# First norm's modulation: the last four k-blocks from rows on VectorE, beside the matrix products on TensorE

## The chip, the cores and the metric

The kernel runs on one core of a Trainium2 chip. The metric is device microseconds (us) of one execution, and the kernel before was run three times: 1737.07 us in the median, 1736.29 the lowest and 1737.78 the highest. One further execution was profiled, and all rows of the trace come from that one.

## The reference

One layer of a diffusion backbone: 256 latent tokens `x` and 256 context tokens `ctx`, each of width 2048. What matters here is the very first step. From a conditioning vector `c` (and, for the context stream, `c_ctx`) six modulation vectors of 2048 come out of one large matrix; the first norm is then scaled and shifted by two of them, and everything after reads the result `h` (or `hc`).

```
mod   = silu(c)     @ w_mod + b_mod          # w_mod: 2048 x 12288
mod_c = silu(c_ctx) @ w_mod + b_mod
sh_a, sc_a, ... = split(mod, 6)
h  = rmsnorm(x,   norm_g[0]) * (1 + sc_a)  + sh_a
hc = rmsnorm(ctx, norm_g[0]) * (1 + csc_a) + csh_a
p  = h @ w_in                                 # and so for hc; the mixer's input projection
```

Behind that come attention and a bidirectional recurrence, their merge, an output projection, and a SwiGLU layer, none of which the change touches.

## The kernel before

All values are fp32. Products that need the accuracy are made of three products each: an operand is split into a high part and a low remainder (ScalarE casts the high part, VectorE subtracts it), and high x high, high x low and low x high are summed in PSUM.

Activations lie transposed: 128 channels of the width on the partitions, tokens along the free side. The width of 2048 is thus 16 *k-blocks* of 128 channels. `hx` holds h of both streams for all k-blocks, with high and low part. For k-block k, `make_h` (lines 196 to 203) multiplies x by the scale column `A1[:, k]` and by the norm's factor (line 200, VectorE), adds the shift column `SH1[:, k]` and casts (line 201, ScalarE), and takes the remainder (line 202, VectorE). So h of a k-block can only be made once its two columns of modulation are there.

**The modulation's products.** `w_mod`'s first third (scale and shift of the first norm, 2048 x 4096 words, 33.5 MB) comes as 32 tiles `wm1` of 1 MB, loaded by `load_w` (lines 98 to 101) on SyncE's queue into a pool with three buffers, `raw`. `GROUPS` says how many k-blocks each group makes: four groups of one, then six of two. A group of one has two tiles, a group of two has four. In line 282 TensorE multiplies a tile with the silu of both conditioning vectors as the stationary operand (32 columns of which two are filled), four contraction blocks in four column strips of the array; the result `pm` is a pair of rows. Those rows must become columns: ScalarE copies them out of PSUM (line 297), TensorE turns them with small products (line 300, `pt`), and VectorE adds the bias and makes `A1` and `SH1` (lines 304 to 306).

**The first blocks.** So that TensorE has other work while the modulation weights come in, six output blocks of the next stage's projection are summed along with it, k-block by k-block (`pre`, `pre_mm`, products of line 144): 18 products for a k-block. Their weights `wst` come in pieces, on SyncE's queue for k-blocks 0 to 3 and on GpSimd's from 4 on (line 224), and are split by `start_operands` (lines 244 to 265), which also calls `make_h`. k-blocks whose number leaves a remainder below 3 when divided by 5 have their split weights in the pool `wH`/`wL`, the others in eight buffers `hC`.

The loop over the groups (lines 267 to 310) takes a group's tiles one by one and puts a share of the waiting first-block products behind each; a group's own k-blocks are lined up for later rounds, and two empty rounds at the end take the rest. `norm_x` (lines 184 to 194) makes the norm's factor of a stream: eight squares on ScalarE, summed on VectorE, and a product with ones on TensorE (line 193, `ssx`).

The written order is not the order that runs: each engine takes its instructions strictly in the order of its queue, and this order is drawn up at build time by a planner, which goes by its own idea of costs and lets whatever is ready first go first, the earlier written one before the later one. Buffers are given out in that same plan. Thus the first-block products of a group run in the trace right behind that group's own turn into columns, one round earlier than they are written.

Later in the kernel 64 further tiles of `w_mod` (`wm2`) are worked off on VectorE by `mod_job` (line 346): there the matrix lies with the output channels on partitions, and one instruction multiplies a row of 2048 with the broadcast vector and sums it.

## Time and profile before

| what | before |
|---|---|
| median of three runs | 1737.07 us |
| the profiled execution, its own time | 1737.94 us |
| its span, first to last instruction | 1736.2 us |
| mean granted clock of TensorE | 0.992 |
| TensorE / VectorE / ScalarE busy | 98% / 63% / 44% |
| read from and written to HBM | 376.03 MB / 6.32 MB |
| modulation tiles of 1 MB, first norm | 32, all on TensorE |

How to read it: the span is divided among engines that run at once, each with its own queue. A busy share says how much of the span an engine had an instruction under way, not that it set the time. Names such as `pre<-hx,wH` are what an instruction writes and reads, "L144" is line 144 of the kernel; line 144 is a helper's, so the name tells which products are meant: `pre` is the first blocks in the stage under study, `ps` the projections behind it. In rows of the timeline and of the chain the first number is the start, the second the length; in groups of instructions the number behind the busy time is the mean duration in ns. An fp32 product that isn't split shows as two instructions.

### The profile page before, as it was taken

To read this page: it belongs to the slowest core of one execution; us is meant where nothing else is said; L and a number is where in the kernel's file an instruction comes from. 1 tells how busy PE (TensorE), PEld (TensorE's weight loads), DVE (VectorE), ACT (ScalarE), POOL (GpSimd) and SP (SyncE) were. 2 spreads that over 40 slices of the span, in tenths; PEclk is the share of its full clock that TensorE was granted. 3 is DMA by queue.
4 is the path that set the end of the run, shared out by engine and by line. 5 is a ranking of instruction groups with operands and counts; after the bars stand their busy time and mean duration, and the time that the engine had idled before them with its cause. 6 is when DMAs were issued, how large, how long until landed. Compare 5 with 4: busy or idle time off the path is not lost.

```text
span 1736.2 us, 22132 instructions
## 1 busy us (share of the span) xinstructions
PE 1695.1 (98%) x8715; PEld 1411.1 (81%) x8715; DVE 1087.9 (63%) x1619; ACT 763.8 (44%) x1086; POOL 53.2 (3%) x81
## 2 busy tenths in 40 slices
PE   6899999999999999999999899999999999999997
PEld 4457888888888888889998788888888888888886
DVE  5336877787778776666765765565455655545456
ACT  5225443333334544445544554444444444344443
POOL 0100000000000000001210000000000000000000
PEclk9899999999999999999999999999999999999999
DMA  9983545555556565587766456665566665555553
GB/s 388 357 325 133 198 165 200 213 194 203 186 180 230 186 252 190 194 308 295 266 230 227 158 218 243 242 234 186 194 241 233 236 231 209 193 193 184 213 193 121
DMA packets 60247, 383.78 MB, mean 221 GB/s; under 512 B 7104, under 2 KB 7920, under 8 KB 16880
## 3 DMA queue, kind: packets, MB, share of 16 engines
q1 hardware_dynamic: 55328, 368.15, 57.7%
q0 software_dynamic: 4096, 13.11, 2.0%
q8 instruction: 68, 1.11, 0.2%
q10 hardware_dynamic: 720, 1.12, 0.2%
q14 instruction: 35, 0.29, 0.0%
HBM read 376.03 MB, written 6.32 MB: 220 GB/s over the span
## 4 chain that ended last, share of the span: by engine, by line
PE 96%; DMA 2%; DVE 1%; ACT 1%; issue 0%; SPq 0%; DVEq 0%; ACTq 0%
PE pst L832 45%; PE ps L144 13%; PE ps L148 11%; PE ps L149 6%; PE psb L767 5%; PE pre L144 4%; DMA raw<-in_wm_dram 1%; PE pm L282 1%; PE pst L926 1%; PE psS L705 1%; PE po L729 1%; PE psS L702 1%; PE pv L677 1%; PE pq L661 1%; PE pk L144 1%; PE pgt L968 1%
## 5 line engine op out<-in xcount | busy, mean ns | idle before, releaser
L110 DVE TENSOR_TENSOR wL<-raw,wH 128x1024 fp32r<-128x1024 f32 x480 | 589.1, 1230 | 480.2 <-ACT wH L108 458.9
L108 ACT CAST wH<-raw 128x1024 fp32r<-128x1024 f32 x480 | 502.6, 1048 | 700.0 <-PE pst L832 390.5
L832 PE MATMUL pst<-wH,hx 128*128 128x512 f32 x2272 | 660.6, 390 | 0.0
L832 PEld LDWEIGHTS pst<-wH,hx 128*128 128x128 f32 x2272 | 425.7, 188 | 87.6
L832 PE MATMUL pst<-wL,hx 128*128 128x512 f32 x1136 | 402.2, 389 | 0.0
L148 PE MATMUL ps<-hx,wH 128*128 128x512 f32 x832 | 298.9, 400 | 0.0
L832 PEld LDWEIGHTS pst<-wL,hx 128*128 128x128 f32 x1136 | 213.2, 188 | 44.4
L149 PE MATMUL ps<-hx,wL 128*128 128x256 f32 x832 | 234.9, 283 | 0.0
L144 PE MATMUL ps<-hx,wH 128*128 128x512 f32 x672 | 212.4, 394 | 0.0
L148 PEld LDWEIGHTS ps<-hx,wH 128*128 128x128 f32 x832 | 156.2, 188 | 36.8 <-issue 1.9
L346 DVE CUSTOM_DVE_ANT_0 raw<-raw,cb 128x2048 f32<-128x2048 f32 x64 | 146.1, 2283 | 29.1 <-DMA raw<-in_wm_dram 29.1
L149 PEld LDWEIGHTS ps<-hx,wL 128*128 128x128 f32 x832 | 157.0, 189 | 3.3 <-DVE mx L707 1.1
L144 PEld LDWEIGHTS ps<-hx,wH 128*128 128x128 f32 x672 | 125.2, 188 | 25.5
L144 PE MATMUL ps<-hx,wL 128*128 128x512 f32 x336 | 132.0, 393 | 0.0
L144 PE MATMUL pre<-hx,wH 128*128 128x512 f32 (+1 forms) x204 | 68.7, 420 | 5.5 <-ACT hx L201 5.3
L144 PEld LDWEIGHTS ps<-hx,wL 128*128 128x128 f32 x336 | 63.2, 188 | 12.6
L144 PEld LDWEIGHTS pre<-hx,wH 128*128 128x128 f32 x204 | 40.6, 209 | 26.5 <-ACT hx L201 12.7
L767 PE MATMUL psb<-hx,wH 128*128 128x256 f32 x256 | 46.8, 283 | 0.0
L767 PE MATMUL psb<-hC,wH 128*128 128x256 f32 x256 | 46.8, 283 | 0.0
L767 PEld LDWEIGHTS psb<-hx,wH 128*128 128x128 f32 x256 | 39.9, 192 | 0.0
L767 PEld LDWEIGHTS psb<-hC,wH 128*128 128x128 f32 x256 | 39.9, 192 | 0.0
L144 PE MATMUL pre<-hx,wL 128*128 128x512 f32 (+1 forms) x102 | 39.5, 390 | 0.0
(258 smaller groups left out, 1416.6 us busy)
## 6 DMA issues: line engine op xcount, KB each, us to landing
raw<-in_wm_dram SPq DMA_DIRECT2D x96, 1024.0 KB, 4.8
raw<-in_wfi_dram SPq DMA_DIRECT2D x88, 1024.0 KB, 4.8
raw<-in_win_dram SPq DMA_DIRECT2D x73, 1024.0 KB, 4.8
raw<-in_wfo_dram SPq DMA_DIRECT2D x44, 1024.0 KB, 4.8
raw<-in_wbr_dram SPq DMA_DIRECT2D x16, 1024.0 KB, 5.5
raw<-in_wout_dram SPq DMA_DIRECT2D x16, 1024.0 KB, 4.8
raw<-in_wqk_dram SPq DMA_DIRECT2D x4, 1024.0 KB, 5.5
sgd<-sgx POOLq DMA_DIRECT2D x16, 256.0 KB, 5.2
```

What stands on the lines that cost most here:

```text
L108: nc.scalar.copy(H, raw[:, o:o + n])
L110: nc.vector.tensor_tensor(L, raw[:, o:o + n], H.bitcast(F32), op=ALU.subtract)
L144: nc.tensor.matmul(o, l, r, start=(first and i == 0), stop=(last and i == len(seq) - 1))
L148: nc.tensor.matmul(ps, w[0], act.rearrange("p e t -> p (e t)"), start=first, stop=False)
L149: nc.tensor.matmul(ps[:, 0:T], w[1], act[:, 0, :], start=False, stop=last)
L282: nc.tensor.matmul(pm[32 * (k % 4):32 * (k % 4) + 32, 0:n], cst[:, k], raw[:, kk * n:(kk + 1) * n], start=(k < 4), stop=(k >= KD - 4))
L346: nc.vector.tensor_tensor_reduce(out=raw, in0=raw, in1=cbt[0], scale=1.0, scalar=0.0, op0=ALU.mult, op1=ALU.add, accum_out=mod2[:, i // KD ...
L661: nc.tensor.matmul(pq[:, i * T:(i + 1) * T], l, r, start=(k == 0 and i == 0 and z == 0), stop=(k == 3 and i == 1 and z == 2))
L677: nc.tensor.matmul(pv[:, i, :], ckvs[:, k, l, ts_], r, start=(i == 0 and k == 0 and z == 0), stop=(i == 1 and k == 1 and z == 2))
L702: nc.tensor.matmul(psS, qn[a][:, i * T + qb * P:i * T + (qb + 1) * P], kn[b], start=(n == 0), stop=False)
L767: nc.tensor.matmul(ps[:, br * T:(br + 1) * T], l, r, start=(br == 0 and k == 0 and z == 0), stop=(br == 1 and k == NH - 1 and z == 2))
L832: mm = nc.tensor.matmul(ps[hf], l, r, start=(k == 0 and n == 0), stop=(k == nk - 1 and n == 2))
```

## The change

The last four k-blocks (12 to 15) of the first norm's modulation leave TensorE. `GROUPS` ends after eight groups, and `KV = 12` is the first k-block done the other way. Their eight tiles (scale and shift, four k-blocks each) are laid out with the output channels on the partitions, so that VectorE can multiply each row with the broadcast vector and sum it, for both streams, in four pieces of 512 columns.

For that the two conditioning vectors must lie on all partitions. `make_creps` makes these copies at the beginning: 32 products with the identity, whose stationary operand is a column of the vector broadcast over 128 columns, and eight copies out of PSUM, by turns on ScalarE and VectorE. The copies take all eight `hC` buffers until the last tile is reduced. So the split weights of k-blocks 3, 4, 8 and 9 go to the space in `hx` that belongs to the k-blocks 13 to 15, which are made last, and the squares of the second norm go to three slices of another tile instead of `hC` buffers.

A tile is loaded and reduced by `vector_mod` behind the last two tiles of each of the groups 3 to 6, and after group 6 `vector_mod_end` sums the four pieces and writes the columns of `A1` and `SH1`. k-blocks 12 and 13, then 14 and 15, are started in two more empty rounds behind group 7. The number and size of the loads stay as they were.

```
-GROUPS = [1, 1, 1, 1, 2, 2, 2, 2, 2, 2]
+GROUPS = [1, 1, 1, 1, 2, 2, 2, 2]
+KV = 12
...
     def norm_x(s):
...
-            sq = acc if q == 0 else ap.tile([P, 512], F32, tag="hC", name="sqx", bufs=8)
+            if q == 0:
+                sq = acc
+            elif s == 0:
+                sq = ap.tile([P, 512], F32, tag="hC", name="sqx", bufs=8)
+            else:
+                o = 512 + (q - 1) % 3 * 512
+                sq = cst_t[:, o:o + 512]
...
+    creps = []
+
+    def make_creps():
+
+        for s in range(2):
+            for q in range(4):
+                ps = pj.tile([P, 512], F32, tag="pj", name="pcr")
+                for i in range(4):
+                    nc.tensor.matmul(ps[:, i * P:(i + 1) * P], cv[:, 4 * q + i, s:s + 1].broadcast_to([P, P]), ident,
+                                     start=(i == 0), stop=(i == 3))
+                t_ = ap.tile([P, 512], F32, tag="hC", name="crep", bufs=8)
+                if q % 2:
+                    nc.vector.tensor_copy(t_, ps)
+                else:
+                    nc.scalar.copy(t_, ps)
+                creps.append(t_)
+
+    vparts = wk.tile([P, 64], F32, name="vparts").rearrange("p (j s q) -> p j s q", j=8, s=2)
+
+    def vector_mod(j):
+
+        raw = load_w(wm1[2 * KV + j])
+        junk = wk.tile([P, 512], F32, tag="f", name="vjunk")
+        for s in range(2):
+            for q in range(4):
+                r = raw[:, q * 512:(q + 1) * 512]
+                nc.vector.tensor_tensor_reduce(
+                    out=r if s else junk, in0=r, in1=creps[4 * s + q], scale=1.0, scalar=0.0, op0=ALU.mult,
+                    op1=ALU.add, accum_out=vparts[:, j, s, q:q + 1])
+
+    def vector_mod_end():
+        m = wk.tile([P, 16], F32, name="vmod")
+        nc.vector.tensor_reduce(m, vparts.rearrange("p j s q -> p (j s) q"), axis=mybir.AxisListType.X, op=ALU.add)
+        m = m.rearrange("p (k a s) -> p k a s", k=4, a=2)
+        nc.vector.tensor_tensor(A1[:, KV:KD, :], m[:, :, 0], bc(bm[:, KD + KV:2 * KD], 2), op=ALU.add)
+        nc.vector.tensor_tensor(SH1[:, KV:KD, :], m[:, :, 1], bc(bm[:, KV:KD], 2), op=ALU.add)
+        nc.vector.scalar_tensor_tensor(A1[:, KV:KD, :], A1[:, KV:KD, :], 1.0, bc(gsm[:, 0, KV:KD], 2),
+                                       op0=ALU.add, op1=ALU.mult)
...
     norm_x(0)
+    make_creps()
+    pre += [pj.tile([P, 512], F32, tag="pj", name=f"pre{i}") for i in range(4)]
+    pre += [px.tile([P, 512], F32, tag="px", name=f"pre{i}") for i in range(4, NPRE)]
...
+        elif k < KV:
+
+            u = [hx[:, k % 5 - 3, 13 + i] for i in range(3)]
+            pr_ = [(wide(u[0]), wide(u[1])), (u[2][:, 0], u[2][:, 1])]
+            for rw, (H_, L_) in zip(parts, pr_):
+                nc.scalar.copy(H_, rw)
+                nc.vector.tensor_tensor(L_, rw, H_.bitcast(F32), op=ALU.subtract)
...
-    for g, nk in enumerate(GROUPS + [0, 0]):
+    for g, nk in enumerate(GROUPS + [0, 0, 0, 0]):
...
             for _ in range(min(share, len(todo))):
                 pre_mm(*todo.pop(0))
+            if 3 <= g < 7 and kt >= nt - 2:
+                vector_mod(2 * (g - 3) + kt - nt + 2)
         todo, held = held, []
         if not nk:
+            k = KV + 2 * (g - len(GROUPS))
+            for kk in range(k, min(k + 2, KD)):
+                held.extend(start_operands(kk))
             continue
...
             (todo if g < 2 else held).extend(start_operands(k))
+        if g == 6:
+            vector_mod_end()
```

The host lays the eight tiles out behind the others, scale before shift for each k-block.

More of the change, by code (lines that the diff above doesn't have):

```diff
@@ L203, in make_h @@
                                            op0=ALU.add, op1=ALU.subtract)
+    creps = []
[30 more added lines that the diff above has]
+                                       op0=ALU.add, op1=ALU.mult)
     NPRE = 6
-    pre = [pj.tile([P, 512], F32, tag="pj", name=f"pre{i}") for i in range(4)]
-    pre += [px.tile([P, 512], F32, tag="px", name=f"pre{i}") for i in range(4, NPRE)]
+    pre = []
     def pre_mm(ws, k, b, s=None):
@@ L1064, in _layout @@
         k0 += nk
+    for k in range(k0, KD):
+        for base in (D, 0):
+            grp.append(wm[:, base + P * k:base + P * (k + 1)].T[None])
     o["wm1"] = np.concatenate(grp)
```

2 lines of the change are left out of this document (added).

## The prediction

> **What bounds the kernel now.** I read the page first, then the busy time of each engine in stretches of 20 us (every column is a busy time with a count, and at the end stand the granted clock, the share of the DMA engines and their rate), then the chain of waits in order of time.
>
> ```profile
> PE 1695.1 (98%) x8715; PEld 1411.1 (81%) x8715; DVE 1087.9 (63%) x1619; ACT 763.8 (44%) x1086; POOL 53.2 (3%) x81
> ```
>
> ```profile
> 20.00:40.00 20.00, 18.30 (x158) 13.60 (x162) 12.81 (x27) 8.51 (x18) 2.28 (x4) 0.91 1.02 416
> 40.00:60.00 20.00, 15.78 (x96) 8.99 (x92) 11.60 (x30) 9.28 (x22) 6.37 (x12) 0.95 1.01 411
> 60.00:80.00 20.00, 18.33 (x88) 10.67 (x81) 6.57 (x18) 4.31 (x10) 2.13 (x4) 0.84 0.85 320
> 80.00:100.00 20.00, 19.18 (x101) 11.47 (x100) 6.33 (x17) 4.89 (x11) 2.13 (x4) 0.95 0.84 321
> 100.00:120.00 20.00, 19.94 (x111) 11.51 (x110) 6.51 (x17) 5.12 (x11) 0.00 (x0) 1.00 0.81 315
> 120.00:140.00 20.00, 17.51 (x93) 11.85 (x92) 9.59 (x24) 6.00 (x11) 1.19 (x2) 0.92 0.84 331
> 140.00:160.00 20.00, 20.00 (x100) 16.31 (x100) 8.71 (x9) 8.21 (x12) 0.71 (x1) 1.00 0.23 86
> ```
>
> TensorE carries the kernel, and from 140 us on it has no hole at all, so whatever the first stage ends earlier the whole kernel ends earlier. The stage that the change touches ends where the first product of the next one (line 148) starts:
>
> ```profile
> 146.52 0.39 PE L144 MATMUL pre<-hx,wL 128*128 128x512 f32 x1
> 146.74 0.39 PE L148 MATMUL ps<-hx,wH 128*128 128x512 f32 x1
> ```
>
> Until 60 us this stage goes at the pace of the transfers (share 1.0, 411 to 416 GB/s); from 60 to 140 TensorE is nearly full and the transfers run at some 320 GB/s. They have room left there because their three buffers are held by waiting products: the queue's own waits are on the modulation products of line 282.
>
> ```profile
> SPq L100 <- PE pm L282: 82.9, 32, 6.6
> ```
>
> So before the change two resources take turns: the transfers first, TensorE after them. The change takes from the second.
>
> **The change part by part.** The chain in order of time (start, length, what) prices TensorE's side:
>
> ```profile
> 112.08 5.48 PE pre L144 x23
> 118.61 4.93 DMA raw<-in_wm_dram
> 123.59 1.06 PE pm L282 x8
> 124.66 6.80 PE pre L144 x29
> 131.46 1.00 PE pm L282 x8
> ...
> 134.28 0.80 PE pt L300 x8
> 135.49 0.50 DVE xt L200
> 136.01 0.92 ACT hx L201 x2
> 136.98 9.93 PE pre L144 x36
> ```
>
> *Removed.* Eight weight tiles lose their products: 1.0 us each (131.46), 8 us. Two groups lose their turn of the rows (line 300): 0.8 us each (134.28), 1.6 us. Together 9.6 us of TensorE. The row copies on ScalarE go too, worth nothing alone, for ScalarE is at a quarter of its time here.
>
> *What stays.* 29 products took 6.80 us, 0.2345 us each. A k-block is 6 blocks times 3 products, so 18 x 0.2345 = 4.2 us.
>
> *Added at the beginning.* 32 small fp32 products, each shown by the trace as two instructions (the ssx products, two in the code, are four in the row). The nearest rows, with start, length and count:
>
> ```profile
> 12.89 2.07 PE L193 MATMUL ssx<-acc,cn 128*128 128x256 f32 x4 [12.89 <-DVE acc L190]
> ...
> 38.16 0.50 PE L300 MATMUL pt<-c,row 128*128 128x2 f32 x4
> ```
>
> Half an ssx instruction, 0.26 us at that place, is the upper bound for 128 columns, a pt instruction, 0.125 us, the lower one: 64 instructions are 8 to 16.6 us. I take 14, for the ssx row has the full width and the same cold start. The vector they read is copied for TensorE at 4.55 us in the rows of VectorE:
>
> ```profile
> 4.55 0.19 DVE L164 COPY cst<-sm 128x32 f32<-128x32 f32 x1
> ```
>
> From 4.6 us TensorE idles until 12.89: 8.3 us are free, and the norm's product comes up to some 6 us late (0 to 8.3; 0 if it goes ahead of the small ones). Does that cost? The chain says what lay behind it:
>
> ```profile
> 14.96 3.04 PE pm L282 x32
> 18.02 11.15 DMA raw<-in_wm_dram
> ```
>
> The load issued at 18.02 when the first products gave their buffer back took 11.15 us to land, while the page's median for these loads is 4.8:
>
> ```profile
> raw<-in_wm_dram SPq DMA_DIRECT2D x96, 1024.0 KB, 4.8
> ```
>
> 6.3 us of queue stood before it. A delay of 6 us is thus covered by transfers that are due anyway; one of 8.3 costs 2. I put it at 0, with 2 as the upper bound. The eight copies out of PSUM (four on ScalarE, four on VectorE) wait beside the squares and sums of the first norm:
>
> ```profile
> L190 DVE TENSOR_TENSOR acc<-acc,sqx 128x512 f32<-128x512 f32 x14 | 9.7, 692 | 1.9 <-ACT sqx L188 0.7
> L462 ACT COPY vn<-pv 128x512 f32<-128x512 f32 x8 | 4.7, 594 | 1.5 <-PE pv L459 1.5
> ```
>
> At 0.69 and 0.59 us they add at most 2.8 and 2.4 us in front of that norm, under the same cover. The second norm's squares go through three buffers where there were eight: ScalarE then follows VectorE's sums, nothing late. The weights of k-blocks 3, 4, 8 and 9 go to other space of the same number of slots: nothing.
>
> *Added on VectorE.* Each of eight tiles is read twice, in four pieces of 512 columns: 64 passes. The same operation at full width:
>
> ```profile
> L346 DVE CUSTOM_DVE_ANT_0 raw<-raw,cb 128x2048 f32<-128x2048 f32 x64 | 146.1, 2283 | 29.1 <-DMA raw<-in_wm_dram 29.1
> L346 DVE DVE_READ_ACCUMULATOR2_ANT mod<- 128x1 f32 x64 | 5.3, 83 | 0.0
> ```
>
> A quarter of 2283 ns is the lower bound, 0.57 us; L190's 0.692 with the 0.083 of the sum's read is the upper one, 0.775. I take 0.65, near L190, the row of the same width: 5.2 us a tile, 41.6 in all (36.5 to 49.6). In 40 to 120 us VectorE was busy 11.60 + 6.57 + 6.33 + 6.51 = 31.0 us. With 41.6 it is 72.6 of 80. It fits, with little left: a tile's passes can stand in front of a group's scale vectors and h on VectorE's queue, TensorE waits for these h with the next modulation products queued behind, and SyncE's loads wait for the buffers of both. GpSimd's loads of first-block weights wait for VectorE's splits and slip with them; they run several k-blocks ahead.
>
> *Moved.* The transfers are as many bytes, but the eight tiles now go between the others, so the last tile for TensorE is still the 32nd of 32, and behind it stand six k-blocks (10 to 15) where two stood. That is the price: six are 6 x 4.2 = 25.3 us. With the last turn and restart I count 27 us from the end of the last modulation product X to the stage's end, where before it was 146.74 - 132.46 = 14.3.
>
> *When is X?* The thirteenth tile came at about 59.1 us before, waited for by TensorE:
>
> ```profile
> 59.20 1.93 PE L282 MATMUL pm<-raw,cst 128*32 128x512 f32 x8 [2.14 <-DMA raw<-in_wm_dram]
> ```
>
> The transfers were full until then, so it comes no earlier after. GpSimd had four pairs of first-block weights still to issue, the first and the last of them:
>
> ```profile
> 67.86 1.06 POOL L224 DMA_DIRECT2D rw<-in_wst_dram  x2 [9.30 <-DVE wL L110]
> ...
> 92.44 1.06 POOL L224 DMA_DIRECT2D rw<-in_wst_dram  x2 [4.28 <-DVE wL L249]
> ```
>
> From there, 19 tiles of 1.049 MB and four k-blocks of first weights of 0.39 MB (128 x 768 words) are 21.5 MB: at 411 GB/s 52 us. TensorE has 14 tiles, three turns and six k-blocks (4 to 9): 14 + 2.4 + 25.3 = 42 us. Three buffers: thirteen tiles for TensorE hold one for 4.8 + 1.0 us, six for VectorE for 4.8 + 5.2, in sum 135 us, 45 for each buffer before any waiting. So transfers bound it, VectorE and the buffers close by. Before, the slowest resource in this stretch was TensorE: 20 tiles, four turns and 173 products (ten k-blocks less seven) are 20 + 3.2 + 40.6 = 63.8 us, and it took 132.46 - 59.2 = 73.3, 15% more. With the same 15%, 52 become 59.8 and X = 119.
>
> TensorE's work in this stretch leaves it some 17 us idle, and the vector k-blocks are ready once the 28th tile is reduced, four loads before X. I let 3 us of their products slip in ahead of X (0 to 6). End: 119 + 27 - 3 = 143, against 146.74: **3.7 us less**. The rest of the kernel is unchanged and follows TensorE.
>
> The profiled execution took 1737.94 us with a span of 1736.2, 0.87 above the median of 1737.07. 1737.07 - 3.7 = **1733.4 us**. A difference under 0.2%, 3.5 us, counts as none.
>
> **The rivals.**
>
> *The transfers stay full (20%).* For it: 411 to 416 GB/s for 40 us when nothing held them. Then X = 59.2 + 52 + 1 = 112.2, 1 us slips in ahead, the end is 138.2: 8.5 us less, 1728.6. Against it: six tiles now hold a buffer for twice as long.
>
> *VectorE's passes become the wait (18%), slower.* The place is a group's turn in groups 4, 5 and 6: h waits for a tile's whole 5.2 us ahead of it on VectorE, TensorE waits for h, both kinds of buffer stay held, and the transfers stand. Three times 5.2 on the 52 are 67.6 us, X = 127, the end 127 + 27 - 3 = 151: 4.3 us more, 1741.4. It decides once X passes 146.7 - 24 = 122.7, a hold of 3.8 us a group. For it: 72.6 of 80 us busy on an engine that takes its work in order. Against it: a group's own VectorE work is short, and a tile's eight passes needn't stand together.
>
> *The beginning gives it back (15%), no difference.* The small products go first at 0.26 us each: the norm's product 8.3 us late, 2 us of it uncovered, and nothing slips in ahead of X: -3.7 + 2 + 3 = 1.3 us more, 1738.4.
>
> *The transfers' 315 to 321 GB/s after 60 us are their own limit (5%), slower.* 21.5 MB at 320 are 67 us, X = 127, the end 151, 4 us more. Against it: the 411 of the stretch before, and the queue's waits on line 282.
>
> The Trainium skill, DMA: Bandwidth & Descriptors, Specifications, puts the HBM limit of one core at about 358 GB/s; by it 21.5 MB would take an estimated 60 us, with the 15% 69, X = 128, and the change would lose some 5 us; the trace disagrees, with 416 and 411 GB/s in 20 to 60 us, and so this rival has no more than its 5%.
>
> **A cold clock** is a cost inside all of them. After the wait of 2.14 us at 59.20 and after 1.91 at 136.98 the next products ran at half pace:
>
> ```profile
> 61.06 3.36 PE L144 MATMUL pre<-hx,wH 128*128 128x512 f32 x7
> ```
>
> 36 products from 136.98 took 9.93 us instead of 8.4, 1.5 lost. TensorE will idle more in the new stretch; four such losses are 6 us on its 42, still under the 52, so I add nothing.
>
> **How the numbers follow.** The forecast has 42%, with its own range from 1730.4 to 1736.4 by the 0 to 6 us that slip in ahead; what lies beyond 3.5 us in it, rather more than half, is 23%, the other 19% count as no difference. The full transfers add 20% to faster, the late beginning 15% to no difference; of VectorE's rival 15% are slower and 3% no difference, and the transfers' own limit is slower. Faster 43%, no difference 37%, slower 20%. The range of 1727.5 to 1741 leaves out the far ends of the full transfers and half of the two slower rivals.
>
> **What would show it.** The first line 148 product near 143 us; DMA share above 0.9 and TensorE clearly under 18 of 20 us in 60 to 110; 25 us of unbroken line 144 products before the end; passes of 0.6 to 0.7 us; the first ssx product at 13 to 21 us with the transfers still full behind it. I am wrong if TensorE waits for h behind VectorE's passes in groups 4 to 6 (then the second rival), if the transfers are still at 320 GB/s while TensorE idles, or if the last modulation product comes after 122.7 us.

## The result: 1.4% slower

| | before | after |
|---|---|---|
| median, runs | 1737.42 us, 4 | 1761.96 us, 4 |
| lowest to highest | 1736.29 to 1737.99 | 1761.3 to 1763.9 |
| the profiled execution, its span | 1736.2 us | 1759.1 us |
| last modulation product ends | 132.46 us | 139.46 us |
| first projection product (`ps`) | 146.74 us | 169.40 us |

The ratio is 1.0144, its 95% interval 1.0126 to 1.0161: 24.5 us lost where 3.7 were to be won, and outside the range. In the profile the first `ps` product comes 22.7 us later and the span is 22.9 us longer, so the whole loss arises in the stage that the change touches.

The page of the changed kernel gives no hint of it: TensorE's share is a point lower.

```profile
PE 1703.9 (97%) x8699; PEld 1422.8 (81%) x8699; DVE 1128.2 (64%) x1749; ACT 764.2 (43%) x1088; POOL 54.9 (3%) x81
```

The stretches of 20 us do; their columns are as before, the last three being the granted clock, the DMA engines' share and GB/s:

```profile
20.00:40.00 20.00, 16.94 (x122) 12.45 (x126) 12.69 (x25) 8.07 (x17) 3.33 (x6) 0.83 0.95 366
40.00:60.00 20.00, 15.57 (x96) 10.62 (x92) 16.95 (x53) 5.84 (x14) 2.21 (x5) 0.83 0.84 311
60.00:80.00 20.00, 8.42 (x42) 4.09 (x35) 11.11 (x34) 3.44 (x8) 3.12 (x6) 0.62 0.97 388
80.00:100.00 20.00, 14.38 (x69) 7.72 (x67) 11.79 (x35) 2.54 (x5) 2.13 (x4) 0.84 0.68 256
100.00:120.00 20.00, 16.35 (x74) 8.98 (x74) 14.76 (x47) 4.14 (x9) 1.06 (x2) 0.77 0.86 322
120.00:140.00 20.00, 16.71 (x76) 9.16 (x76) 17.57 (x52) 7.65 (x17) 1.06 (x2) 0.83 0.82 299
```

TensorE is busy 8.42 of 20 us in 60 to 80 and never over 17. That would be as forecast if the transfers were full beside it. In 60 to 80 they nearly are, with 388 GB/s; after that they are not: 256 GB/s in 80 to 100, less than before the change. And in 20 to 60, where they ran at 416 and 411 GB/s before, they now run at 366 and 311. VectorE isn't full either, with 11 to 18 of 20 us. No engine bounds this stretch; something that all of them wait for does.

The same view over one stretch, from 20 us to the first `ps` product, for the kernel before and then for the changed one:

```profile
20.00:146.74 126.74, 115.77 (x658) 73.57 (x659) 53.41 (x130) 40.21 (x85) 14.80 (x26) 0.93 0.86 339
```
```profile
20.00:169.40 149.40, 115.64 (x578) 75.58 (x579) 91.96 (x257) 38.81 (x82) 14.82 (x26) 0.82 0.75 287
```

This is the balance of the change. 80 products went (8 tiles of 8 and 2 turns of 8), the forecast's 9.6 us. Yet TensorE is busy just as long, 115.64 against 115.77 us: the clock fell from 0.93 to 0.82, and the products that stayed took 9.5 us longer. Idle time rose from 10.97 to 33.76 us, by 22.8. So -9.6 of work, +9.5 of cold clock, +22.8 of idleness make +22.7.

Two places of idleness. The chain of waits of the changed kernel, start, length and what:

```profile
59.39 1.90 PE pm L340 x16
...
61.31 9.93 DMA raw<-in_wm_dram
...
71.28 1.98 PE pm L340 x8
...
77.69 7.62 PE pre L145 x24
...
90.48 1.04 PE pm L340 x8
91.52 0.02 issue
91.54 8.06 DMA raw<-in_wm_dram
...
99.62 0.69 DVE vjunk L238
...
105.72 2.93 PE pre L145 x6
...
115.08 1.04 PE pm L340 x8
116.12 0.02 issue
116.14 5.31 DMA raw<-in_wm_dram
...
121.47 0.69 DVE vjunk L238
```

The three loads were issued late, behind a modulation product that gave its buffer back, and are waited for to their landing. The first is the fourth tile of group 4 and is TensorE's. The other two are VectorE's tiles, and the chain goes on through their first passes, which stand on VectorE's queue in front of that group's scale vectors or h. The end of the stage, in the rows of TensorE:

```profile
138.40 1.06 PE L340 MATMUL pm<-raw,cst 128*32 128x512 f32 x8
140.23 1.05 PE L363 MATMUL pt<-c,row 128*128 128x2 f32 x8 [0.76 <-ACT row L360]
143.19 3.35 PE L145 MATMUL pre<-hx,wH 128*128 128x512 f32 x7 [1.91 <-ACT hx L208]
...
169.40 0.39 PE L149 MATMUL ps<-hx,wH 128*128 128x512 f32 x1
```

29.9 us from the end of the last modulation product to the next stage, with all 108 first-block products of six k-blocks in it.

Why are the loads late? The SyncE queue's own waits up to 145 us (in total, times, longest), and the rows of the tile `raw` between 59.2 and 139.5 us:

```profile
SPq L101 <- PE pm L340: 53.3, 22, 5.8
SPq L101 <- DMA raw<-in_wm_dram: 26.8, 9, 6.3
SPq L101 <- DVE vparts L238: 24.6, 5, 10.2
SPq L101 <- DVE A L367: 6.2, 1, 6.2
```
```profile
L101 SPq DMA_DIRECT2D raw<-in_wm_dram x19: 327/328/350, 60.5 to 130.6; - x19
...
DMA to landing us min/median/max: 4.7/6.9/10.3
```

19 loads in 70.1 us, 3.9 us apart: with three buffers, one turn of a buffer from a load to the next is 11.7 us. The same rows of the kernel before:

```profile
L100 SPq DMA_DIRECT2D raw<-in_wm_dram x17: 327/328/328, 61.2 to 122.2; - x17
...
DMA to landing us min/median/max: 4.6/5.7/8.7
```

17 loads, 3.8 us apart. The pace of the loads, which the change was to speed up, stayed the same, while two more of them fell into the stretch.

### The profile page after: what moved, and what is told of

The parts are those of the page before. It is cut to its first block, busy times and chain, and to the rows that moved or that the text cites. A ratio compares the mean times of both kernels' runs of the same rounds, so it can differ in the third digit from the quotient of the medians.

```text
span 1759.1 us, 22238 instructions
## 1 busy us (share of the span) xinstructions
PE 1703.9 (97%) x8699; PEld 1422.8 (81%) x8699; DVE 1128.2 (64%) x1749; ACT 764.2 (43%) x1088; POOL 54.9 (3%) x81
## 4 chain that ended last, share of the span: by engine, by line
PE 95%; DMA 2%; DVE 1%; ACT 1%; issue 0%; SPq 0%; DVEq 0%; ACTq 0%
PE pst L897 45%; PE ps L145 13%; PE ps L149 11%; PE ps L150 6%; PE psb L832 5%; PE pre L145 4%; DMA raw<-in_wm_dram 1%; PE pm L340 1%; PE pst L991 1%; PE psS L770 1%; PE po L794 1%; PE psS L767 1%; PE pv L742 1%; PE pq L726 1%; PE pk L145 1%; PE pgt L1033 1%
## 5 line engine op out<-in xcount | busy, mean ns | idle before, releaser
L411 DVE CUSTOM_DVE_ANT_0 raw<-raw,cb 128x2048 f32<-128x2048 f32 x64 | 146.1, 2282 | 29.7 <-DMA raw<-in_wm_dram 29.5
L145 PE MATMUL pre<-hx,wH 128*128 128x512 f32 (+1 forms) x156 | 51.1, 411 | 6.9 <-ACT hx L208 6.9
L145 PEld LDWEIGHTS pre<-hx,wH 128*128 128x128 f32 x156 | 31.4, 211 | 18.7 <-ACT hx L208 9.4
L340 PE MATMUL pm<-raw,cst 128*32 128x256 f32 (+1 forms) x256 | 29.7, 570 | 16.1 <-DMA raw<-in_wm_dram 16.1
```

The costliest lines, as they stand in the source:

```text
L145: nc.tensor.matmul(o, l, r, start=(first and i == 0), stop=(last and i == len(seq) - 1))
L340: nc.tensor.matmul(pm[32 * (k % 4):32 * (k % 4) + 32, 0:n], cst[:, k], raw[:, kk * n:(kk + 1) * n], start=(k < 4), stop=(k >= KD - 4))
L411: nc.vector.tensor_tensor_reduce(out=raw, in0=raw, in1=cbt[0], scale=1.0, scalar=0.0, op0=ALU.mult, op1=ALU.add, accum_out=mod2[:, i // KD ...
```

## Theories and experiments

*Theory*: the three buffers bound the stretch (landing, waiting in an engine's queue, use), and TensorE, in its fixed order, idles, and its clock falls; the end and the beginning add their own loss. *Rivals*: VectorE's passes alone; TensorE's order drawn up by the planner; the small products at the beginning.

All runs, with the profiled execution's end of the last modulation product, first `ps` product, and TensorE's busy and idle time from 20 us to it (busy from the row of the stretches, idle the rest). The ratio is to the kernel before, run again beside each batch of kernels. Its medians there lie between 1737.42 and 1738.88 us, so two rows of different batches can differ by up to 1.5 us for that alone. The last columns come from one execution each: that of e11 took 3.9 us more than its median, that of e19 2.5 more, that of e15 1.5 less.

| kernel | median us | ratio to before, 95% | last `pm` | first `ps` | busy, idle |
|---|---|---|---|---|---|
| after | 1761.96 | 1.0126 to 1.0161 | 139.5 | 169.40 | 115.6, 33.8 |
| e1_own_buffers | 1752.54 | 1.0063 to 1.0096 | 130.1 | 160.31 | 113.1, 27.2 |
| e2_two_passes | 1758.42 | 1.0096 to 1.0126 | 134.9 | 164.88 | 113.9, 31.0 |
| e6_short_hold | 1759.34 | 1.0105 to 1.0135 | 136.2 | 167.37 | 115.8, 31.6 |
| e7_own_two_passes | 1745.84 | 1.0034 to 1.0064 | 124.2 | 154.12 | 111.6, 22.6 |
| e3_copies_alone | 1743.45 | 1.0017 to 1.0041 | 137.8 | 152.18 | 117.9, 14.3 |
| e11_moved_alone | 1739.70 | 1.0007 to 1.0024 | 135.6 | 151.50 | 116.7, 14.8 |
| e4_interleaved | 1747.36 | 1.0035 to 1.0065 | 138.2 | 155.52 | 112.7, 22.9 |
| e9_interleaved_three | 1758.59 | 1.0106 to 1.0132 | 149.2 | 166.27 | 118.2, 28.1 |
| e8_interleaved_own | 1743.45 | 1.0020 to 1.0044 | 133.6 | 150.41 | 107.8, 22.6 |
| e13_own_two_interleaved | 1745.30 | 1.0028 to 1.0052 | 134.9 | 153.86 | 113.8, 20.1 |
| e12_late_copies | 1742.74 | 1.0016 to 1.0039 | 135.9 | 149.96 | 113.9, 16.1 |
| e10_two_blocks | 1757.88 | 1.0098 to 1.0132 | 143.0 | 166.82 | 118.3, 28.5 |
| e14_even_order | 1760.22 | 1.0113 to 1.0147 | 140.5 | 170.10 | 113.9, 36.2 |
| e18_inter_even | 1746.21 | 1.0027 to 1.0061 | 137.5 | 154.78 | 108.8, 25.9 |
| e19_own_even | 1748.69 | 1.0048 to 1.0078 | 128.2 | 159.26 | 116.9, 22.3 |
| e15_own_inter_even | 1736.11 | 0.9981 to 1.0003 | 125.7 | 142.99 | 106.8, 16.2 |
| e16_own_inter_even_late | 1741.83 | 1.0010 to 1.0028 | 132.1 | 149.16 | 113.4, 15.7 |
| e17_before_even | 1736.96 | 0.9988 to 1.0007 | 129.3 | 144.28 | 114.8, 9.5 |

### Buffers or passes

**Own buffers.** Seven of the eight VectorE tiles go to space that is free by then (slices of `cst_t` and `kr`, and the first quarter of both `xs`), each in two loads; the second stays in `raw`.

```
-        raw = load_w(wm1[2 * KV + j])
+        raw = load_own(j)
```

> The changed kernel, but seven of the eight vector tiles are loaded into two buffers of their own (a free slice with the space of kr, and the first k-blocks of x once their h is made), so that the three raw buffers serve TensorE's tiles; VectorE's passes are the same. Theory 'buffers' (a vector tile keeps one of three buffers for 5 to 10 us after landing, and the transfers stand): the last modulation product comes at 115 to 122 us instead of 139.4, DMA share above 0.9 from 60 to 110 us, 1735 to 1745 us in all against 1762. Rival 'VectorE's queue' (its passes stand in front of the groups' h, whoever owns the buffers): within 5 us of the changed kernel, 1757 to 1762.

**Fewer passes**: one piece of the four is multiplied and summed. **Short hold**: all eight passes run, but only the first of each tile reads it.

```
-            for q in range(4):
+            for q in range(1):
```

> The changed kernel with two of the eight passes on each vector tile; the other six are left out, and their part of the modulation with them. Loads and products stay. 'Buffers' and 'VectorE's queue' both expect most of the loss back: 1735 to 1742 us. Rival 'order' (eight tiles loaded between the others and six k-blocks left for the end cost it, whatever VectorE does): 1752 to 1762.

```
-                    out=r if s else junk, in0=r, in1=creps[4 * s + q], scale=1.0, ...
+                    out=junk, in0=creps[7 - 4 * s - q] if s + q else r, in1=creps[4 * s + q], scale=0.0 if s + q else 1.0, ...
```

> The changed kernel, but only the first of the eight passes reads the vector tile; the other seven are made on the resident copies of the vectors and scaled by zero, so that the tile's buffer is free after one pass while VectorE is as busy as before. It leaves out seven eighths of the vector k-blocks' modulation. 'Buffers': 1735 to 1745 us, the queue's waits on the passes nearly gone. 'VectorE's queue': 1755 to 1762 us, since 4.9 us of passes a tile still stand on it.

Own buffers give 9.4 us back, a quarter of the passes 3.5, the short hold 2.6 (10.9, 5.0 and 4.1 against the kernel before of their own batch). None met the theory of the buffers as it was expected: e1 lies between the theory's range and the rival's, e2 in the range of "order", e6 in that of VectorE's queue. So VectorE's passes alone are not the cause, neither by the time that they hold a buffer nor by their work; sharing the buffers is the larger part, and one remedy alone doesn't bring the loss back.

The edits of e1 and e2 in one kernel:

> Buffers of their own for the vector tiles and only two of the eight passes (the other six and their part of the modulation are left out). Theory 'loads held in two ways' (three buffers too few, then VectorE too full): both are lifted, the last modulation product comes at 113 to 120 us, the transfers stay above 390 GB/s to 110 us, and with six k-blocks behind it the total is 1737 to 1743. Rival 'TensorE's order' (its own tiles wait behind a k-block's products whatever VectorE does): the last product at 126 us or later, 1748 to 1753.

Both together: 16.1 us, more than 9.4 and 3.5, and the last modulation product ends at 124.2 us, 5 us from the forecast's 119 and behind the 113 to 120 expected; the time lies between the two ranges. With buffers and passes lifted the stretch up to that product runs nearly as forecast; still this kernel is 8 us slower than before, for the end behind that product stays 30 us.

### The beginning

The small products, copies and moved buffers with all 32 tiles on TensorE, as before the change:

```
-GROUPS = [1, 1, 1, 1, 2, 2, 2, 2]
+GROUPS = [1, 1, 1, 1, 2, 2, 2, 2, 2, 2]
...
-            if 3 <= g < 7 and kt >= nt - 2:
-                vector_mod(2 * (g - 3) + kt - nt + 2)
```

> All sixteen k-blocks on TensorE as before, plus the small products, the eight copies and the moved buffers of the change; no vector tile. Theory 'the beginning is free' (the transfers cover the small products): within 3 us of the kernel before. Rival 'the beginning costs': the transfers fall from 416 to about 366 GB/s in 20 to 40 us as in the changed kernel, and the stage ends 5 us later or more.

The same without the small products and copies (left out of e3):

```
-    make_creps()
```

> This kernel is e3_copies_alone without the small products and their eight copies: all 32 modulation tiles are on TensorE as before the change, only the moved buffers of the change remain (the second norm's squares in three slices, the split weights of k-blocks 3, 4, 8 and 9 in the space of h). Theory that the 5 us at the beginning come from the small products and copies, which change the order that the planner draws up for the groups behind them: 1736.5 to 1738.5 us, as before the change, first projection product (ps) at 146 to 148 us and the fifth modulation tile used at about 29 us. Rival, that the moved buffers cost it (fewer slices for the squares, so the second norm is late): 1741 to 1744 us, as e3_copies_alone, with the fifth tile at 33 to 34 us.

The beginning costs 5.5 us with the small products and 1.7 without (ratios 1.0029 and 1.0016, whose intervals overlap a little), so neither theory was right alone: the moved buffers have a small part, the products and copies probably the larger one. How they cost it shows in the fifth modulation tile. The first row is of `e11_moved_alone`, where it stands behind the second turn as before the change; the second of `e3_copies_alone`, where it stands behind 18 first-block products:

```profile
28.94 1.07 PE L339 MATMUL pm<-raw,cst 128*32 128x256 f32 x16 [0.35 <-DMA raw<-in_wm_dram]
```
```profile
33.49 1.07 PE L340 MATMUL pm<-raw,cst 128*32 128x256 f32 x16
```

Its buffer comes free 4.5 us later, and the transfers, at 416 and 411 GB/s before the change, run at 360 and 365:

```profile
20.00:40.00 20.00, 16.57 (x126) 11.72 (x126) 12.66 (x25) 8.10 (x18) 3.33 (x6) 0.91 0.96 360
40.00:60.00 20.00, 17.71 (x108) 9.78 (x108) 9.47 (x24) 7.10 (x16) 5.15 (x10) 0.91 0.97 365
```

### The end

k-blocks 12 to 15 are started one by one, each behind the group in which its two tiles are reduced.

```
-        if g == 6:
-            vector_mod_end()
+        if 3 <= g < 7:
+            vector_mod_end(g - 3)
+            held.extend(start_operands(KV + g - 3))
```

> The changed kernel with the vector k-blocks finished one at a time, k-block 12 behind group 3 and so on, so that their products stand between the groups and two k-blocks instead of six are left for the end; three raw buffers as in the changed kernel. 'Buffers': the last modulation product stays near 139 us, but only some 14 us follow it instead of 30, so 1744 to 1750. 'VectorE's queue': four h's more between the passes, the last modulation product moves to 145 us or later, 1750 to 1760. If neither holds and the end alone costs ('order'): 1738 to 1744.

In this kernel h of the k-blocks from 13 on overwrites split weights of k-blocks 3 and 4, in part before their products; the amount and kind of the work are the same. The next one puts these weights elsewhere. In both, and in all kernels below that start VectorE's k-blocks one by one, the split weights from k-block 5 on are all in `wH`/`wL`.

> This kernel is the changed kernel with k-blocks 12 to 15 started one by one behind groups 3 to 6, as soon as their two tiles are reduced, instead of all behind the last group; the three buffers stay shared. It differs from e4_interleaved only in the place of the split weights of k-blocks 3 and 4. Theory that the end alone is worth 14 us: 1746 to 1749 us, first ps at 154 to 157, some 17 us from the last modulation product to it. Rival, that what is put ahead at the end only fills TensorE where the loads wait and X moves later by as much: 1755 us or more.

14.6 us back in the one, 3.4 in the other, which differs from it in the place of two weights. For the second the theory failed and its rival held: the last modulation product moves to 149.2 us. Its queue waits for the small closing sums (29.6 us in total, 12.2 in e4) in place of the passes:

```profile
SPq L101 <- PE pm L343: 54.3, 21, 6.1
SPq L101 <- DVE vmod L247: 29.6, 4, 10.2
SPq L101 <- DMA raw<-in_wm_dram: 25.6, 11, 6.7
```

The place also decides which products must wait for which h. With it the planner draws up another order, on VectorE and on TensorE alike, and a tile's buffer then comes free later. These two kernels don't show the order apart from the place; the even order below does, on the second of them.

Interleaving (starting the k-blocks one by one) with the own buffers of e1, and that with the one piece of e2 besides:

> Vector k-blocks finished one at a time behind groups 3 to 6, and seven of the eight vector tiles in buffers of their own; the whole computation. If the two remedies add up (9 us from the buffers, 15 from the end): 1735 to 1740. If VectorE, busy 18.5 of 20 us with the own buffers, then sets the pace: 1742 to 1750.

> This kernel is e8_interleaved_own with two passes per VectorE tile instead of eight (a quarter of each row is multiplied and summed, the other three quarters are left out). It lifts both holds and the end. Theory of three separate losses (beginning 5 us, holds, end): only the beginning is left, the last modulation product ends at 124 to 128, first ps at 142 to 147, 1734 to 1738 us. Rival, that with the end interleaved TensorE's own work and its order set the time, so that the passes no longer matter: as e8_interleaved_own, 1742 to 1745 us.

Interleaved with own buffers: 1743.5 us. With a quarter of the passes besides: no better, against the theory of three separate losses. It seems that without the even order below what is saved in one place is given back in another. e8's time lies where it was expected if VectorE set the pace, but e15 below is faster with VectorE just as busy (18.23 of 20 us in 60 to 80 in both), so VectorE didn't set it.

```
-    make_creps()
...
+            if g == 3 and kt == 0:
+                make_creps()
             if 3 <= g < 7 and kt >= nt - 2:
```

The results of the small products also move to another pool of PSUM (`px` for `pj`).

> This kernel is e8_interleaved_own with the small products and copies written in the middle of the group loop, just ahead of the first VectorE tile, instead of the beginning; they run between first-block products. Theory that their place at the beginning cost 5 us: the fifth modulation tile comes at about 30 to 31 us, the first ps product 4 to 5 us earlier than in e8_interleaved_own, at 145 to 147, 1736 to 1739 us in all, no different from before the change. Rival, that it is their work on TensorE, some 10 us wherever it stands, once TensorE is the slower side: no earlier than e8_interleaved_own, 1743 to 1746 us.

The small products written in the middle of the loop bring nothing that can be measured (1742.7 against 1743.5): the fifth tile is at 31.29 us, near the 30 to 31 expected, but the 32 products, TensorE's and the copies' work, now stand among the first-block products.

```
-GROUPS = [1, 1, 1, 1, 2, 2, 2, 2]
-KV = 12
+GROUPS = [1, 1, 1, 1, 2, 2, 2, 2, 2]
+KV = 14
```

> Only k-blocks 14 and 15 by VectorE: four vector tiles, one in each of the groups 3 to 6, nine groups on TensorE, four k-blocks behind the last modulation product. 'The end' (what stands behind the last product costs 4.2 us a k-block, half as many more as in the change) and a loss in proportion: 1748 to 1752. 'Buffers': one vector tile a group leaves two for TensorE all the time, and most of the loss goes: 1739 to 1744.

Two k-blocks on VectorE instead of four lose 20 us, nearly as much as four, and more than either theory expected. The loss isn't proportional to the moved work.

### The order on TensorE

What was left was the order. In the queue of the changed kernel up to 24 first-block products stand in front of a modulation tile (in others up to 38). One rule keeps the first-block products behind the tile that they are written behind, and a group's own are written one round earlier:

```
+                with tc.issue_after(mm.ins):
                     pre_mm(*todo.pop(0))
...
-            (todo if g < 2 else held).extend(start_operands(k))
+            todo.extend(start_operands(k))
```

> This kernel is the changed kernel with one more rule for the order of TensorE's queue: the first-block products that are written behind a modulation tile aren't put in front of it, and a group's own first-block products are written one round earlier. So 6 to 9 of them, 18 at most, stand between two modulation tiles of a group instead of up to 32. From 20 us to the first ps product the changed kernel takes 149.4 us, of which TensorE is busy 115.6 and idle 33.8. Theory that long runs of first-block products in front of a modulation tile hold its buffer, so that loads start late and TensorE idles later: idle falls by 8 us or more, first ps at 156 to 162 us, 1749 to 1755 us in all. Rival, that the three buffers are held by landing and VectorE's passes whatever TensorE's order: idle within 4 us of 33.8, first ps at 165 to 172, 1758 to 1764 us.

> This kernel is e8_interleaved_own (own buffers for VectorE's tiles, its k-blocks started one by one) with the even order of e14_even_order: first-block products aren't put in front of the modulation tile ahead of which they weren't written. Theory that the planner's uneven order is what is left there: TensorE's idle time from 20 us to the first ps product falls from 22.6 to 14 to 18 us, first ps at 143 to 147, 1735 to 1739 us. Rival, that the order only moves the idle time about: 148 to 152 us, 1741 to 1746 us.

> This kernel is e15_own_inter_even with the small products and copies written in the middle of the group loop, as in e12_late_copies, so that the first groups run as before the change. Theory that order and beginning add up: first ps at 141 to 145 us, 1732 to 1737 us in all, at least as fast as before the change. Rival, that the small products between first-block products put back what their absence at the beginning gives: 145 to 150 us, 1738 to 1743 us.

> This kernel is the kernel before the change with the even order alone; all 32 modulation tiles stay on TensorE. It is the control for the even order: what order alone does without the change. Before, TensorE idles 11.0 us from 20 us to the first ps product, at 146.74. Theory that an uneven order costs where buffers are the narrow place, and less where TensorE is nearly full: first ps at 143 to 148 us, 1734 to 1739 us. Rival, that an even order is a gain or a loss of its own of the same size as in the changed kernel: under 1732 or over 1742 us.

> This kernel is e15_own_inter_even with the three buffers shared again: VectorE's k-blocks started one by one, even order on TensorE, no own buffers. Theory that with three shared buffers neither order nor an interleaved end can help much, since landing and passes hold the buffers (e14_even_order: nothing from the order alone): first ps at 155 to 167 us, between e4 and e9, 1747 to 1759 us. Rival, that order and interleaved end are enough and own buffers are not needed: 143 to 149 us, 1736 to 1741 us.

> This kernel is e15_own_inter_even with VectorE's four k-blocks all behind the last group again, as in the change: own buffers and even order, no interleaving. Theory that the end is then the narrow place: the last modulation product comes at 118 to 124 us, about where the forecast put it, the first ps product some 30 us later, at 147 to 153, 1740 to 1746 us. Rival, that the order brings as little as in e14_even_order: last modulation product at 129 to 131 and first ps at 158 to 161 us, as in e1_own_buffers, 1750 to 1753 us.

By itself the even order brings next to nothing (e14, 1760.2), as its rival said, and nothing to the kernel before either (e17). It helps most where VectorE's k-blocks are started one by one: 12.4 us with three buffers (e9, 1758.6, to e18, 1746.2) and 7.3 us with own buffers (e8, 1743.5, to e15, 1736.1); with own buffers and the k-blocks at the end it is 3.9 us (e1 to e19). So with three buffers, too, the order is part of the loss. The traces of the kernels with three buffers show where (worked out as in the table of the next section): from landing to use TensorE's tiles waited 4.3 us in the mean in e9 and 1.8 in e18, but in the changed kernel 2.5 and in e14 1.5, where landing took 0.5 us longer. The eight kernels with each of the three remedies or without it:

| median us | VectorE's k-blocks at the end | one by one |
|---|---|---|
| planner's order, three buffers | 1762.0 | 1758.6 |
| planner's order, own buffers | 1752.5 | 1743.5 |
| even order, three buffers | 1760.2 | 1746.2 |
| even order, own buffers | 1748.7 | 1736.1 |

In the planner's order both other remedies together give 18.5 us, and starting one by one alone only 3.4. With the even order they add up: own buffers are worth 11.5 and 10.1 us, starting the k-blocks one by one 14.0 and 12.6, both 24.1. Each does it at its own place: own buffers bring the last modulation product from 140.5 to 128.2 and from 137.5 to 125.7; starting one by one brings the `ps` product from 29.7 to 17.3 and from 31.0 to 17.3 us behind it. e18 came just under the theory's range of 1747 to 1759. For e19 it named the right place, the end, but the last modulation product came at 128.2, behind the 118 to 124 expected, and the kernel 3 us over its range.

In `e15_own_inter_even` the forecast's picture stands, from 20 us to the first `ps` product and in 60 to 100 us:

```profile
20.00:142.99 122.99, 106.75 (x578) 68.87 (x579) 93.35 (x269) 37.66 (x82) 14.83 (x26) 0.92 0.86 342
...
60.00:80.00 20.00, 14.79 (x66) 7.59 (x65) 18.23 (x61) 3.20 (x7) 1.46 (x3) 0.74 1.02 418
80.00:100.00 20.00, 20.00 (x104) 13.19 (x103) 18.64 (x59) 6.00 (x13) 2.13 (x4) 1.00 1.02 420
```
```profile
124.62 1.07 PE L356 MATMUL pm<-raw,cst 128*32 128x512 f32 x8
...
142.99 0.39 PE L149 MATMUL ps<-hx,wH 128*128 128x512 f32 x1
```

Transfers full at 418 and 420 GB/s, VectorE at 18 of 20 us beside them, the same 578 products of TensorE in 106.75 us where the changed kernel took 115.64, and the first `ps` product at 143. It is the fastest form of the change, 25.9 us better than the change as made, and not measurably better than the kernel before (0.9992, 0.9981 to 1.0003), nor than the kernel before with the even order alone (e17, 1736.96 in the same batch). The late copies, on top of it, lose 5.7 us: e16's theory fell.

## Why the prediction was wrong, point by point

**The bound of the kernel** was read rightly in effect. "No hole at all" is too strong (TensorE idles 5.5 us between 146.74 and 1720 us before the change), but what the stage lost the kernel lost, 22.7 of 22.9 us.

**Removed, 9.6 us**: right. 80 products fewer, and at nearly the clock of before (e15, 0.92 against 0.93) TensorE needs 106.75 us where it needed 115.77.

**Beginning, cost 0 (0 to 2)**: the size of the work was overrated, its cost missed. The products took 10.3 us, not 14, and the first `ssx` product came at 15.06, within the 13 to 21 foreseen:

```profile
4.56 6.47 PE L220 MATMUL pcr<-c,sm 128*128 128x128 f32 x32 [4.56 <-DVE sm L161]
11.39 3.84 PE L220 MATMUL pcr<-c,sm 128*128 128x128 f32 x32 [0.36 <-DVE crep L224]
15.06 1.03 PE L200 MATMUL ssx<-acc,cn 128*128 128x256 f32 x4
```

But the cover, "transfers that are due anyway", was itself lost: a modulation tile slipped behind 18 products in the planner's order and held a buffer. Measured alone (e3), the beginning costs 5.5 us, 1.7 of them by the moved buffers. In the changed kernel the thirteenth load landed at 62.89 us, before at 59.06. So the sum's start, the thirteenth tile that "comes no earlier after", was already 3.8 us off, the other way.

**Passes of 0.65 us, 5.2 a tile**: right. 0.685 us each, the read of the sum lies beside the next one, and they follow one another at 0.61 us.

**The three buffers, the step that failed**: "Three buffers: thirteen tiles for TensorE hold one for 4.8 + 1.0 us, six for VectorE for 4.8 + 5.2, in sum 135 us, 45 for each buffer before any waiting. So transfers bound it." 135 us over 19 tiles are 7.1 us a tile; the runs showed 11.7. The trace gives the parts, when each load is put together with the products or passes on its tile, in the order of the queue (means in us, loads from the fourteenth on; a tile is held from the load's issue to the end of its use):

| | landing | waiting | use | held |
|---|---|---|---|---|
| forecast, TensorE's 13 tiles | 4.8 | 0 | 1.0 | 5.8 |
| changed kernel, TensorE's 13 | 6.7 | 2.5 | 1.4 | 10.5 |
| forecast, VectorE's 6 | 4.8 | 0 | 5.2 | 10.0 |
| changed kernel, VectorE's 6 | 7.6 | 0.5 | 6.4 | 14.5 |
| before, TensorE's 19 | 6.2 | 3.7 | 1.1 | 11.0 |

In sum 224 us, 74.6 for each buffer instead of 45, in the 79.0 us from the first of these loads (60.45) to X: the buffers were held for 94% of the time. A shorter use alone doesn't free them: in e6 VectorE's tiles are held for 8.0 us, but TensorE's then for 12.6, 4.1 of them waiting, and X comes only 3.3 us earlier. Buffers of their own for VectorE's tiles bring 9.4 to 15.1 us in each of the four pairs of kernels above, and with all three remedies the transfers are full in 60 to 100 us (e15). So the shared buffers, with what they wait for, bound the stretch, and not the transfers. Of the 88 us that the sum lacked, 41 are landing, for which it took the page's 4.8, the median of all 96 loads of the kernel; 35 are waiting, put at nothing, nearly all of it that of TensorE's tiles in its queue; 12 are use, as other work lies between a tile's passes. The row for it was quoted: the queue's waits on line 282, 6.6 us at most. They were read as room, because TensorE was full; they were the buffers' limit, and the pace of the loads stayed at 3.9 us. X came at 139.5 us instead of 119, and behind the 122.7 that the prediction set as the point at which it would be wrong. Own buffers move it by 9.4 us (e1) to 15.6 (e9 to e8), and buffers and passes together to 124.2 (e7).

**The 15% on top of the bound** was taken from TensorE's slack before and put on transfers, whose loss is of another kind; 59.8 us became 80.3 from 59.2 to X.

**Cold clock, nothing added**: wrong. It was excused by the time that TensorE was idle anyway, but first-block products behind a wait can stand in front of the next modulation tile, and then a slow pace holds its buffer: the 24 products at 77.69 took 7.62 us, 0.32 each instead of 0.2345, and a tile that landed as they began was used at 85.25. In the stretch it cost 9.5 us, the whole saving. The last wait of the stage shows it: behind 0.76 and 1.91 us of idleness, with eight small products between, seven products took 3.35 us, 0.48 each instead of 0.2345. Waits for a transfer do the same: behind the load that landed at 71.2 a tile's eight products took 1.98 us instead of 1.0. The Trainium skill, TensorE: Matmul & The Clock Gate, in the section "HAM oscillation — how this bites in real kernels", describes work in bursts shorter than the wait for the next transfer, which starts cold every time; the trace agrees, with a clock of 0.62 in 60 to 80 us.

**The end, 27 us less 3**: 29.9 and nothing slipped ahead. The sum left 1.7 us for the last turn and the restart, where its own rows gave 4.5 before (132.46 to 136.98) and the changed kernel took 3.7 (139.46 to 143.19). The k-blocks of VectorE were ready too late, and in the written order they all stand behind the last group. That six k-blocks lie behind X was priced; that 12.6 to 14.0 us were avoidable, by starting the k-blocks one by one in the even order, was not seen.

**The second rival** (18%, 4.3 us) named the place, and its point, X past 122.7, was passed. VectorE's rows show it in the changed kernel: between the first step of the scale vectors (line 367) and the first step of h (line 207) stand four passes:

```profile
101.58 0.15 DVE L367 TENSOR_TENSOR A<-pt,sm 128x4 f32<-128x4 f32 x1
101.66 0.15 DVE L368 TENSOR_TENSOR SH<-pt,sm 128x4 f32<-128x4 f32 x1
101.72 0.68 DVE L238 CUSTOM_DVE_ANT_0 vjunk<-raw,crep 128x512 f32<-128x512 f32 x1
...
103.63 0.69 DVE L238 CUSTOM_DVE_ANT_0 raw<-raw,crep 128x512 f32<-128x512 f32 x1
104.24 0.08 DVE L238 DVE_READ_ACCUMULATOR2_ANT vparts<- 128x1 f32 x1
104.24 0.48 DVE L207 SCALAR_TENSOR_TENSOR xt<-xt,A,rstd 128x256 f32<-128x256 f32 x1
```

Its size was far smaller than its sum of 5.2 us a group: in group 5 the turn ended at 100.90 and the next first-block products began at 105.72, where before 1.9 us lay between (93.77 to 95.68), so h came some 2.9 us late; in group 6 it was some 0.8 us, in group 4 none. Taking six of the eight passes away gave back 3.5 us of 24.5 (e2). It is not the main loss. The rival of the transfers' own limit fell: 418 and 420 GB/s in e15. So did, as made, the rival of full transfers. The rival of the beginning (15%) named a real loss, but put 2 us of it uncovered where 5.5 were measured.

**What stays open.** Why two k-blocks on VectorE lose nearly as much as four (e10) was not settled. Why fewer passes bring nothing once own buffers and interleaving are there (e13) was not either; both were run without the even order, and e4 and e9 show that another place for two weights, and the order that follows from it, makes 11 us of difference there. Why TensorE's tiles wait so much longer in e9 than in the changed kernel, and so what the even order can win, wasn't traced further. That the small products cost by the order that they upset, and not by their time on TensorE and the copies, is argued from one tile's place, not shown apart.

## What to carry to other kernels

Before work moves to another engine, reckon each buffer's whole turn (landing in a burst, waiting in an in-order queue, use) from the stretch itself: the measured distance of the loads times the number of buffers is that turn, and if it doesn't get shorter, no engine's relief makes the stage faster. Give the moved tiles buffers of their own, start what hangs on them as soon as each is ready, and keep long runs of other work from standing in front of the instruction that frees a buffer: here these made 25.9 us of difference, and alone 9.4, 3.4 and 1.7. Then ask whether the best form wins anything: here the first `ps` product came 3.75 us earlier in one profiled execution, the fastest of ten, 2.5 of which the even order gave without the change (e17), and in the median nothing measurable was won.

## What the runs showed of the hardware

The same number of TensorE instructions (578 or 579) took 106.75 us in this stage at a mean granted clock of 0.92 (e15), 113.1 at 0.84 (e1) and 118.2 at 0.82 (e9): idle time that lowers the clock costs again in the products behind it. Loads of 1 MB that land in 4.8 us in the median of the whole kernel took 6.9 in the median and 10.3 at most in the changed stretch, where two or three are often under way at once, and 5.7 and 8.7 in the same stretch before. And 418 to 423 GB/s were reached beside a VectorE that was busy 18 of 20 us (e15 and, with 423 in 80 to 100 us, e19).
